# A gather for 144 tokens instead of 128, and the order of head 0's projections

## The chip, the cores and the metric

The kernel runs on one core of a Trainium2 chip. The metric is device time in microseconds (us) of one execution; the median of three executions of the kernel before is 3711.65 us (3703.98 to 3716.35). Engines go by the profile's names: PE is TensorE's matmul stream and PEld its weight loads, DVE is VectorE, ACT ScalarE, POOL GpSimd, SP SyncE.

## The reference

512 tokens of width 1024 pass through two blocks in fp32. Block one: convolution mixers, cross attention to 256 memory tokens, and a mixture of 16384 one-neuron experts:

```
q = h @ w_pq                          # 8 heads, two halves of 128
top 16 of each half's 128 scores; top 16 of their 256 sums -> expert_idx, gates
act = gelu(u[expert_idx] . h) * gates # 128 experts per token, rows of 1024
out = sum(act * v[expert_idx])
```

Block two puts 16 meta tokens in front (528 tokens) and runs a gated feed-forward layer, a hybrid mixer and a second feed-forward layer. The mixer has retention (4 heads, decayed scores) and sparse attention, whose keys are chosen by an index score: eight index heads of width 64, `sum_h w_h * relu(iq_h . ik)`, top 128 per query.

## The kernel before, in words

**Weights.** Every product of activations and weights is three matmuls (high times high, high times low, low times high). `_plan` lists all weight blocks of 1 MB in order of use. SP loads a block into one of three buffers (`wraw`, line 76); `_split` makes the high half on ScalarE (`whi`, line 95) and the low half on VectorE or GpSimd (`wlo`, line 96), each with two buffers. `K.mm` (line 175) issues the matmuls at line 184; weights are the stationary operand, tokens the moving one. One block is 16 steps of 3 matmuls.

**The list in the background.** Work of the other engines is put as pairs of a cost and a function into `K.bg`. After each step `K.step` (line 127) adds `K.rate` (times the share of 512 tokens that the matmul had) to a balance, and runs functions while it is positive. Costs are thus only a planned order; `flush` runs all that is left. `hold` and `wait` put an empty entry with a cost there.

**The experts.** The first NS = 128 tokens gather their experts' rows; for the other ND = 384 all experts are computed and most gates are zero. Dense part: `u_block` (line 888) multiplies 256 experts' first-layer rows with the 384 tokens, followed by GELU. 64 such blocks are 16 groups. The first 12 groups (spilled) run while the routing is still being done, and go to DRAM (`AD`, line 1080). Then, for each of the four last groups, `_peer_order` gives a fused pair (first layer, then second) and three second layers of spilled groups, which are reloaded (`back`, `reload`, lines 1099 to 1108): 4 first-layer and 16 second-layer groups, each of 4 blocks of 48 matmuls. `weigh` (line 1093) multiplies activations with the gates and splits them (lines 1096, 272, 274); `v_group` adds to the residual (line 1133). The gates come from `four` (line 1030): one-hot matrices of 4 tokens built on GpSimd, VectorE and ScalarE, and 4 matmuls (line 1058); `gather` (line 1046) brings 16 tokens' gates to DRAM (`GD`).

**The gathered tokens.** `_Gathered` (line 795) holds the 128 tokens with one token per partition. `rows_of_h` transposes their activations (line 811). 128 times per layer, `read` (line 819) issues an indirect DMA of one row per token (128 x 4 KB) on GpSimd's queue, and `step` (line 830) multiplies: for u a product with a sum per token (line 836), for v a scaled addition into `sum` (line 844). Four row buffers, two rows read ahead. These 256 steps stand in the list: `among` (line 847) puts EARLY = 30 + 30 + 38 among the `four`s of the three later token tiles, `more` (line 858) adds PACE = 2.4 per block of a first layer, 1.45 (and one more in a first block) where a spilled group is reloaded, 3.4 in other second layers. `finish` transposes `sum` back before the last group.

**Order on GpSimd's queue.** GpSimd issues, in program order, the row gathers, the reloads and the gates' loads, and builds most of the one-hots. Three buffers of `a` take the reloads; the fourth reload waits for the first to be weighed.

**The mixer around the change.** `_retention` (line 1302) projects the keys of head 0, the index key, the first four heads' index queries (w_iq[0], `proj` at line 1403, rope at line 1406), then half of head 0's values (line 1402, `_values` at line 1286), the other four's, and per head the query (line 1427), values, decayed scores (`inner`, line 1441), their product with the values (line 1464), gates and an output product. `index(i, hp)` (line 1355, 16 calls of 6 small matmuls, 2 relus and 2 sums) and 48 `drop`s (line 1376) stand in the list. Three PSUM accumulators (`mm`) serve projections, values and index products alike. After head 0's values the list is emptied down to its last 52 entries (line 1435):

```
for b in range(2):
    if b:
        values(0)
    o = proj(HQ)
```

Of the kernel before, what the change touches and what calls it, by code (L numbers as in the profile page):

```python
# [18 lines left out]
P = 128  # L19
D = 1024  # L20
# [10 lines left out]
NS = 128  # L31
# [5 lines left out]
EARLY = (30, 30, 38)  # L37
PACE = (2.4, 1.45, 3.4)
# [346 lines left out]
def _plan(d):  # L385
# [47 lines left out]
    add(d["w_iq"][0], True)  # L433
    add(d["w_rv"][0], True)
    add(d["w_iq"][1], True)
    for h in range(4):
        add(d["w_rq"][h], True)
        for n in ("w_rv", "w_rg"):
            for b in range(2):
                if (n, h, b) != ("w_rv", 0, 0):  # L440
                    add(d[n][2 * h + b], True)
# [353 lines left out]
class _Gathered:  # L795


    def __init__(self, K, tp, H):
        self.K, self.tp, self.H = K, tp, H
# [3 lines left out]
    def rows_of_h(self):  # L803

        nc = self.K.nc
        box = self.K.tp.tile([P, T2], F32, name="acc", tag="acc", bufs=1)
        self.gate, self.dots, self.index = box[:, :P], box[:, P:2 * P], box[:, 2 * P:3 * P].bitcast(U32)
        o = self.K.ps.tile([P, 1024], F32, name="mm", tag="mm", bufs=3)
        for k in range(KT):
            for i in range(2):  # L810
                nc.tensor.matmul(o[:, k * P:(k + 1) * P], self.H[i][:, k, :NS].bitcast(F32), self.K.ident, start=i == 0, stop=i == 1)
        nc.scalar.activation(self.h, o, AF.Copy)

    def begin(self, i, j):
        self.K.nc.vector.scalar_tensor_tensor(self.index, i, float(P), j, op0=OP.mult, op1=OP.add)  # L815
        for _ in range(NROW - 2):
            self.read()

    def read(self):
        n = self.nread  # L820
        if n == 2 * P:
            return
        t = self.tp.tile([P, D], F32, name="row", tag="row", bufs=NROW)
        src = self.K.d["u_rows"] if n < P else self.K.d["v_rows"]
        self.K.nc.gpsimd.indirect_dma_start(out=t, out_offset=None, in_=src,  # L825
                                            in_offset=bass.IndirectOffsetOnAxis(ap=self.index[:, n % P:n % P + 1], axis=0))
# [3 lines left out]
    def step(self):  # L830
        n, nc = self.ndone, self.K.nc
        s = n % P
        self.ndone += 1
        t = self.rows.pop(n)
        if n < P:
            nc.vector.tensor_tensor_reduce(t, t, self.h, 1.0, 0.0, OP.mult, OP.add, self.dots[:, s:s + 1])  # L836
            if s == P - 1:
# [464 lines left out]
def _retention(K, tp, H, HQ, R, RT, roots, BIAS, YD, w):  # L1302
    nc, tc = K.nc, K.tc
    with tc.tile_pool(name="ret", bufs=1) as rp:
# [95 lines left out]
        for b in range(2):  # L1400
            if b:
                values(0)
# [444 lines left out]
```

## Time and profile before

| | |
|---|---|
| median of three executions | 3711.65 us |
| the profiled execution | 3718.03 us, its span 3716.3 us |
| TensorE, VectorE, ScalarE, GpSimd busy | 97%, 63%, 38%, 32% of the span |
| weight loads busy | 88% |
| granted clock of TensorE, mean | 0.983 |
| DMA traffic | 583.37 MB, 157 GB/s |

The profile is one execution. A group of instructions has a line of the kernel, an engine, an operation, tiles out<-in, a count, busy time, the mean of one, and what ended the idle time before it. A wait names who waited for whom. The clock is the share of full speed granted to TensorE in a stretch. Matmuls are pipelined, so the duration of one is longer than the pitch from one to the next.

### The profile page before, as it was taken

The numbers are of one execution on the slowest core, as the hardware profiler recorded it, in microseconds if no ns is written. First come the engines' busy times: TensorE is split into PE (matmuls) and PEld (weight loads), VectorE is DVE, ScalarE is ACT, GpSimd is POOL, SyncE is SP. The second block draws the span as 40 slices with busy tenths as digits, with TensorE's granted clock in tenths as the row PEclk, the third lists the DMA queues.
The fourth block names the chain that finished last, engine by engine and source line by source line (L and its number), as shares of the span: only waits on it lengthen the run. The fifth ranks groups of instructions, "written<-read, shape, count | busy, mean of one in ns | idle before, by whom it ended". The sixth has DMA issues, their size and how long they took to land. (4 is left out here: it accounts for less than half of the span.)

```text
span 3716.3 us, 51006 instructions
## 1 busy us (share of the span) xinstructions
PE 3596.8 (97%) x20457; PEld 3269.4 (88%) x20457; DVE 2323.2 (63%) x4126; ACT 1422.8 (38%) x2306; POOL 1179.2 (32%) x940
## 2 busy tenths in 40 slices
PE   8999999998999999999999999989999999999998
PEld 6888788898999899989999999978898889888887
DVE  7896734698888868877887433457534254563334
ACT  4223434235677733323234222333333355442223
POOL 1002323304899934343530100032334333301001
PEclk9999999999999999999999999999999999999999
DMA  3223222236899988888884222231222221332221
GB/s 140 91 102 131 97 102 80 93 118 212 290 298 313 345 302 325 308 293 291 309 320 162 91 91 91 63 111 47 72 83 83 100 88 66 120 111 91 92 101 57
DMA packets 155261, 583.37 MB, mean 157 GB/s; under 512 B 12704, under 2 KB 64032, under 8 KB 112912
## 3 DMA queue, kind: packets, MB, share of 16 engines
q1 hardware_dynamic: 51456, 345.21, 26.5%
q0 software_dynamic: 46576, 190.34, 14.2%
q10 hardware_dynamic: 56992, 44.57, 3.7%
q8 instruction: 161, 2.64, 0.3%
q14 instruction: 76, 0.62, 0.1%
HBM read 527.63 MB, written 52.43 MB: 156 GB/s over the span
## 5 line engine op out<-in xcount | busy, mean ns | idle before, releaser
L184 PE MATMUL mm<-h,whi 128*128 128x512 f32 (+2 forms) x6944 | 1796.4, 351 | 14.4 <-ACT h L380 7.3
L184 PEld LDWEIGHTS mm<-h,whi 128*128 128x128 f32 x6944 | 1195.9, 190 | 146.5 <-ACT h L380 7.3
L184 PE MATMUL mm<-h,wlo 128*128 128x512 f32 (+2 forms) x3472 | 1134.7, 350 | 18.3 <-DVE wlo L96 17.3
L95 ACT ACTIVATE whi<-wraw 128x512 fp32r<-128x512 f32 (+2 forms) x648 | 654.6, 1041 | 524.9 <-PE mm L184 261.2
L184 PEld LDWEIGHTS mm<-h,wlo 128*128 128x128 f32 x3472 | 626.1, 190 | 89.7 <-DVE wlo L96 21.3
L96 DVE TENSOR_TENSOR wlo<-wraw,whi 128x512 fp32r<-128x512 f32 (+2 forms) x387 | 563.5, 1461 | 211.5 <-ACT whi L95 210.9
L96 POOL TENSOR_TENSOR wlo<-wraw,whi 128x512 fp32r<-128x512 f32 (+1 forms) x261 | 436.9, 1696 | 800.7 <-ACT whi L95 765.1
L184 PE MATMUL mm<-w,whi 128*128 128x384 f32 x2048 | 530.4, 340 | 1.4 <-ACT whi L95 1.2
L184 PEld LDWEIGHTS mm<-w,whi 128*128 128x128 f32 x2048 | 376.7, 190 | 2.6 <-ACT whi L95 1.9
L184 PE MATMUL mm<-w,wlo 128*128 128x384 f32 x1024 | 349.5, 341 | 21.0 <-DVE wlo L96 21.0
L1223 POOL TENSOR_TENSOR sl<-sl,r 128x528 f32<-128x528 f32 (+1 forms) x44 | 57.2, 1314 | 732.8 <-ACT sl L1221 732.8
L1037 POOL TENSOR_SCALAR p<-iota,it 128x128 f32<-128x128 f32 x256 | 253.1, 1000 | 44.5 <-ACT whi L95 31.9
L825 POOL DMA_INDIRECT row<-v_rows,acc x128 | 193.1, 1509 | 209.0 <-DVE sum L844 173.5
L184 PE MATMUL mm<-g,whi 128*128 128x264 f32 (+2 forms) x1080 | 226.4, 318 | 0.0
L825 POOL DMA_INDIRECT row<-u_rows,acc x128 | 164.2, 1283 | 176.7 <-DVE acc L815 108.2
L184 PEld LDWEIGHTS mm<-w,wlo 128*128 128x128 f32 x1024 | 194.9, 190 | 25.2 <-DVE wlo L96 25.2
L198 PE MATMUL mm<-whi,h 128*128 128x256 f32 x960 | 181.7, 285 | 7.4 <-DVE tmp L1261 2.6
L844 DVE SCALAR_TENSOR_TENSOR sum<-row,acc,sum 128x1024 f32<-128x1024 f32 x127 | 162.9, 1282 | 33.3 <-DMA row<-v_rows,acc 31.2
L184 PEld LDWEIGHTS mm<-g,whi 128*128 128x128 f32 x1080 | 166.8, 188 | 15.0
L836 DVE CUSTOM_DVE_ANT_0 row<-row,hrow 128x1024 f32<-128x1024 f32 x128 | 156.8, 1232 | 28.2 <-DMA row<-u_rows,acc 28.0
L272 ACT ACTIVATE w<-a 128x384 fp32r<-128x384 f32 x128 | 63.6, 526 | 262.9 <-DVE a L1096 259.2
L198 PEld LDWEIGHTS mm<-whi,h 128*128 128x128 f32 x960 | 151.7, 190 | 9.9 <-DVE v L1295 2.9
(376 smaller groups left out, 4414.5 us busy)
## 6 DMA issues: line engine op xcount, KB each, us to landing
wraw<-uT SPq DMA_DIRECT2D x64, 1024.0 KB, 6.9
wraw<-v SPq DMA_DIRECT2D x64, 1024.0 KB, 7.3
wraw<-w_in SPq DMA_DIRECT2D x27, 1024.0 KB, 4.8
gd<-gc ACTq DMA_DIRECT2D x24, 1024.0 KB, 10.0
g<-gd POOLq DMA_DIRECT2D x16, 1536.0 KB, 8.9
wraw<-ffn_w_gate SPq DMA_DIRECT2D x22, 1024.0 KB, 4.7
wraw<-ffn_w_up SPq DMA_DIRECT2D x22, 1024.0 KB, 4.7
ad<-a ACTq DMA_DIRECT2D x48, 384.0 KB, 7.1
```

The source lines that it names most:

```text
L95: self.nc.scalar.activation(hi[:, a:a + m], t[:, a:a + m], AF.Copy)
L96: eng.tensor_sub(lo[:, a:a + m], t[:, a:a + m], hi[:, a:a + m].bitcast(F32))
L184: self.nc.tensor.matmul(o, a[:, k, (c0 + c) * P:(c0 + c + 1) * P], b[:, k0 + k, lo:hi], start=first and k == 0 and i == 0, stop=last and k ...
L198: self.nc.tensor.matmul(out, x, y, start=start and i == 0, stop=stop and i == 2)
L272: self.nc.scalar.activation(dst[0], src, AF.Copy)
L825: self.K.nc.gpsimd.indirect_dma_start(out=t, out_offset=None, in_=src, in_offset=bass.IndirectOffsetOnAxis(ap=self.index[:, n % P:n % P + ...
L836: nc.vector.tensor_tensor_reduce(t, t, self.h, 1.0, 0.0, OP.mult, OP.add, self.dots[:, s:s + 1])
L844: nc.vector.scalar_tensor_tensor(self.sum, t, self.dots[:, s:s + 1], self.sum, op0=OP.mult, op1=OP.add)
L1037: eng.tensor_scalar(p2[:, j], IOTA, IT[1][:, t:t + 1], None, op0=OP.is_equal)
L1223: nc.gpsimd.tensor_mul(sl[c], sl[c], R)
```

## The change

NS becomes 144: 16 tokens more (NX) gather, and the dense part runs over 368 tokens. The 16 tokens have 16 x 128 expert rows; these are laid out as 128 partitions x 16 (SLOTS), eight partitions per token, so that one gather of 128 rows brings eight rows for each of the 16 tokens; 16 jobs per layer are added to 128, which makes 288 in all, in the order u of the 128 tokens, u of the 16, v of the 128, v of the 16. `begin_rest` sends the indices and gates of the 16 tokens through DRAM into that layout (four DMAs on GpSimd's queue, after the second token tile is routed). `rows_of_h(1)` repeats each of the 16 tokens eight times (ScalarE) and transposes again; `fold` adds the sum of the 128 tokens before the last 16 jobs, and `finish` adds up the eight partitions of each token with eight matmuls. EARLY, PACE and the rate while the spilled groups run are set anew.

In the mixer both index queries are projected in a row, and both halves of head 0's values follow the retention query, as in the other heads: the first half right behind it, the second behind the decayed scores. The plan's order of weights follows.

```
-NS = 128
+NS = 144
+NX = NS - 128
+SLOTS = 8 * 16 * NX // 128
-EARLY = (30, 30, 38)
-PACE = (2.4, 1.45, 3.4)
+EARLY = (30, 30, 40)
+PACE = (2.6, 1.85, 3.8)
...
+        self.jobs = [("u", 0, s) for s in range(P)] + [("u", 1, s) for s in range(SLOTS)]
+        self.jobs += [("v", 0, s) for s in range(P)] + [("v", 1, s) for s in range(SLOTS)]
...
+            if part:
+                for i in range(2):
+                    x[i] = K.temp().rearrange("p (k t) -> p k t", k=4)
+                    nc.scalar.activation(x[i].rearrange("p k (t h) -> p k t h", t=NX),
+                                         self.H[i][:, k0:k0 + 4, P:NS].bitcast(F32).unsqueeze(3).to_broadcast([P, 4, NX, P // NX]), AF.Copy)
...
+    def begin_rest(self, i, j, v, t):
+        nc = self.K.nc
+        d = self.K.dr.tile([2, NX, P], F32, name="rest")
+        nc.vector.scalar_tensor_tensor(t, i, float(P), j, op0=OP.mult, op1=OP.add)
+        nc.gpsimd.dma_start(d[0], t[:NX].bitcast(F32))
+        nc.gpsimd.dma_start(d[1], v[:NX])
+        for n, x in enumerate((self.index[1].bitcast(F32), self.gate[1])):
+            nc.gpsimd.dma_start(x, d[n].rearrange("t (h k) -> (t h) k", k=SLOTS))
...
+        if last and part == 0:
+            self.K.bg[:0] = [(0.3, lambda: self.rows_of_h(1))] if kind == "u" else [(2.0, lambda: None), (0.5, self.fold)]
...
-        while self.due >= 1 and self.planned < 2 * P:
+        while self.due >= 1 and self.planned < len(self.jobs):
...
+    def finish(self):
+        K, nc = self.K, self.K.nc
+        self.more(len(self.jobs))
+        K.flush()
+        a = K.aux()[:, :KT * NX].rearrange("p (k t) -> p k t", k=KT)
+        for k in range(KT):
+            nc.tensor.matmul(a[:, k], self.sum[:, k * P:(k + 1) * P], self.group, start=True, stop=True)
+        x = self.X[:, :, P:NS]
+        nc.vector.tensor_add(x, x, a)
...
+                if t == 1:
+                    rest.begin_rest(box[0], box[1], box["v"].rearrange("p h k -> p (h k)"), small("ix", U32, "t9"))
...
-            K.rate, K.fine, K.late = 0.64, True, True
+            K.rate, K.fine, K.late = 0.66, True, True
...
         for b in range(2):
-            if b:
-                values(0)
             o = proj(HQ)
...
             if b == 0:
-                K.wait(K.us(8.0))
+                K.wait(K.us(11.0))
...
-            values(0 if h else 1)
+            values(0)
...
-            if h:
-                values(1)
+            values(1)
```

## Rows read from the trace of the kernel before

**Rows 1.** The page, its first part: busy time, share of the span, instructions.

```profile
PE 3596.8 (97%) x20457; PEld 3269.4 (88%) x20457; DVE 2323.2 (63%) x4126; ACT 1422.8 (38%) x2306; POOL 1179.2 (32%) x940
```

**Rows 2.** Windows by stage, all engines (the first line names the columns).

```profile
core 0: us, PE busy (x) PEld busy (x) DVE busy (x) ACT busy (x) POOL busy (x), PEclk, DMA share, GB/s
764.00:887.00 123.00, 113.37 (x657) 110.96 (x656) 116.66 (x447) 49.87 (x88) 2.44 (x2) 0.99 0.40 138
887.00:1305.00 418.00, 403.59 (x2508) 398.21 (x2507) 350.01 (x861) 299.03 (x703) 374.97 (x354) 0.98 0.91 308
1305.00:2024.00 719.00, 689.55 (x3853) 682.64 (x3851) 570.22 (x670) 237.91 (x261) 268.61 (x220) 0.98 0.80 293
2441.50:2562.00 120.50, 105.22 (x574) 85.49 (x573) 75.39 (x143) 38.69 (x82) 32.60 (x24) 0.87 0.17 60
```

**Rows 3.** Windows of line 184 alone (PE, PEld, clock, DMA): widths 384, then 264.

```profile
1382.20:1482.80 100.60, 100.60 (x578) 100.60 (x577) 1.00 0.89 328
2100.00:2400.00 300.00, 300.00 (x2465) 300.00 (x2464) 1.00 0.26 87
```

**Rows 4.** Chain of waits, matmuls of width 512: start, us, what.

```profile
3340.58 359.51 PE mm L184 x1569
```

**Rows 5.** Groups of TensorE and VectorE, 887 to 1305 us: count, busy us, mean ns.

```profile
L1058 PE MATMUL aux<-p,p 128*128 128x128 f32 x768 | 109.4, 282 | 14.4 <-issue 7.8 <-DVE p L1042 3.1 <-POOL p L1037 3.1
L836 DVE CUSTOM_DVE_ANT_0 row<-row,hrow 128x1024 f32<-128x1024 f32 x98 | 121.1, 1235 | 22.7 <-DMA row<-u_rows,acc 22.5
```

**Rows 6.** TensorE in order of time where the list is flushed.

```profile
1301.03 3.98 PE L1058 MATMUL aux<-p,p 128*128 128x128 f32 x16 [6.09 <-issue]
```

**Rows 7.** Waits, 1305 to 2024 us, VectorE's and one of TensorE's: total, times, longest.

```profile
DVE a L1096 <- DMA a<-ad: 54.0, 11, 7.3
DVE wlo L96 <- ACT whi L95: 42.4, 38, 4.9
DVE sum L844 <- DMA row<-v_rows,acc: 31.2, 13, 5.9
DVE row L836 <- DMA row<-u_rows,acc: 5.5, 3, 3.7
PE mm L184 <- DVE wlo L96: 27.9, 16, 3.1
```

**Rows 8.** Groups of VectorE, 1305 to 2024 us: count, busy us, mean ns.

```profile
L96 DVE TENSOR_TENSOR wlo<-wraw,whi 128x2048 fp32r<-128x2048 f32 x80 | 183.1, 2289 | 42.5 <-ACT whi L95 42.4
L844 DVE SCALAR_TENSOR_TENSOR sum<-row,acc,sum 128x1024 f32<-128x1024 f32 x127 | 162.9, 1282 | 33.3 <-DMA row<-v_rows,acc 31.2
L274 DVE TENSOR_TENSOR w<-a,w 128x384 fp32r<-128x384 f32 x128 | 66.1, 557 | 11.8 <-ACT w L272 5.9
L1096 DVE TENSOR_TENSOR a<-a,g 128x384 f32<-128x384 f32 x128 | 65.4, 553 | 54.0 <-DMA a<-ad 54.0
L1133 DVE TENSOR_TENSOR X<-X,mm 128x384 f32<-128x384 f32 x126 | 63.8, 548 | 1.2 <-PE mm L184 1.1
```

**Rows 9.** Who waited for line 811's matmuls: us, times.

```profile
  ACT hrow L812: 5.3, 1
```

**Rows 10.** Window of the third second-layer group, which has no reload; columns as in rows 2.

```profile
1449.20:1482.80 33.60, 33.60 (x195) 33.60 (x194) 26.52 (x28) 8.60 (x7) 16.38 (x13) 1.00 0.90 338
```

**Rows 11.** Waits of TensorE, 2441.5 to 2562 us.

```profile
PE aux L198 <- DVE tmp L1449: 3.0, 1, 3.0
PE mm L198 <- DVE tmp L1261: 2.6, 1, 2.6
```

**Rows 12.** Groups, 2441.5 to 2562 us: the index matmuls and their sums.

```profile
L198 PE MATMUL mm<-ik,iq 64*128 64x128 f32 (+3 forms) x96 | 13.5, 377 | 6.7 <-DVE iq L1267 3.8 <-ACT iq L1265 2.9
L1369 DVE SCALAR_TENSOR_TENSOR sc<-rel,iw,sc 128x128 f32<-128x128 f32 (+3 forms) x28 | 17.4, 620 | 8.5 <-ACT rel L1365 6.6
```

**Rows 13.** Windows in the mixer, columns as in rows 2.

```profile
2500.00:2518.00 18.00, 18.00 (x81) 11.63 (x81) 11.58 (x21) 6.24 (x17) 4.73 (x3) 0.81 0.35 133
2544.00:2562.00 18.00, 17.78 (x61) 15.10 (x61) 3.63 (x10) 3.85 (x8) 0.00 (x0) 0.53 0.00 0
```

More of the change, by code (lines that the diff above doesn't have):

```diff
@@ L432, in _plan @@
     add(d["w_i"])
-    add(d["w_iq"][0], True)
-    add(d["w_rv"][0], True)
-    add(d["w_iq"][1], True)
+    for b in range(2):
+        add(d["w_iq"][b], True)
     for h in range(4):
@@ L795, with __init__ @@
 class _Gathered:
-    def __init__(self, K, tp, H):
-        self.K, self.tp, self.H = K, tp, H
+    def __init__(self, K, tp, H, X):
+        self.K, self.tp, self.H, self.X = K, tp, H, X
         self.h = tp.tile([P, D], F32, name="hrow", tag="hrow")
         self.rows, self.nread, self.ndone, self.planned, self.due = {}, 0, 0, 0, 0.0
[L803 to L811, printed above, removed]
+        self.jobs = [("u", 0, s) for s in range(P)] + [("u", 1, s) for s in range(SLOTS)]
+        self.jobs += [("v", 0, s) for s in range(P)] + [("v", 1, s) for s in range(SLOTS)]
@@ new lines, in rows_of_h @@
+    def rows_of_h(self, part=0):
+        nc, K = self.K.nc, self.K
+        if part == 0:
+            box = K.tp.tile([P, T2], F32, name="acc", tag="acc", bufs=1)
+            cut = [0, P, 2 * P, 3 * P] + [3 * P + i * SLOTS for i in (1, 2, 3)]
+            a = [box[:, x:y] for x, y in zip(cut, cut[1:])]
+            self.gate, self.dots, self.index = (a[0], a[3]), (a[1], a[4]), (a[2].bitcast(U32), a[5].bitcast(U32))
+            self.group = K.tp.tile([P, NX], F32, name="group")
+            nc.vector.tensor_reduce(self.group, K.ident.rearrange("p (t h) -> p t h", t=NX), AX.X, OP.add)
+        else:
+            self.h = self.tp.tile([P, D], F32, name="hrow", tag="hrow")
+        o = K.ps.tile([P, 1024], F32, name="mm", tag="mm", bufs=3)
+        for k0 in range(0, KT, 4):
+            x = [h[:, k0:k0 + 4, :P].bitcast(F32) for h in self.H]
+            if part:
[3 more added lines that the diff above has]
+                                         self.H[i][:, k0:k0 + 4, P:NS].bitcast(F32).unsqueeze(3).to_broadcast([P, 4, NX, P // NX]), AF.Copy)
+            for k in range(4):
+                for i in range(2):
+                    nc.tensor.matmul(o[:, (k0 + k) * P:(k0 + k + 1) * P], x[i][:, k], K.ident, start=i == 0, stop=i == 1)
@@ L819, in read @@
     def read(self):
         n = self.nread
-        if n == 2 * P:
+        if n == len(self.jobs):
             return
+        kind, part, s = self.jobs[n]
         t = self.tp.tile([P, D], F32, name="row", tag="row", bufs=NROW)
-        src = self.K.d["u_rows"] if n < P else self.K.d["v_rows"]
-        self.K.nc.gpsimd.indirect_dma_start(out=t, out_offset=None, in_=src,
-                                            in_offset=bass.IndirectOffsetOnAxis(ap=self.index[:, n % P:n % P + 1], axis=0))
+        self.K.nc.gpsimd.indirect_dma_start(out=t, out_offset=None, in_=self.K.d[kind + "_rows"],
+                                            in_offset=bass.IndirectOffsetOnAxis(ap=self.index[part][:, s:s + 1], axis=0))
@@ L863, in more, with fold @@
             self.due -= 1
-    def finish(self, X):
+    def fold(self):
         K, nc = self.K, self.K.nc
-        self.more(2 * P)
-        K.flush()
         for i in range(2):
@@ L885, in _peer @@
         HR = [x[:, :, NS:] for x in H]
[L886 removed]
+        rest = _Gathered(K, tp, H, X)
         def u_block(c_outer=True):
@@ L1070, in _peer @@
                 fours = [(1.1, lambda tb=tb, q=q: four(tb, q))
-                         for tb in range((t * P - NS) // TCH, ((t + 1) * P - NS) // TCH) for q in range(TCH // 4)]
+                         for tb in range(max(t * P - NS, 0) // TCH, ((t + 1) * P - NS) // TCH) for q in range(TCH // 4)]
                 if t < 3:
```

36 lines of the change are left out of this document (19 added, 17 removed).

## The prediction

> **What bounds the kernel now.** The first part of the page shows TensorE busy in 3596.8 of 3716.3 us [rows 1], so a gain has to come out of its matmuls or its few waits, and what matters is which engine it waits for in the two places that the change touches. The windows by stage cut these out [rows 2]. From 764 to 887 us (first three groups of the expert layer, with the routing) VectorE is busy 116.7 of 123 us. From 887 to 1305 us (the other nine spilled groups) TensorE is busy 403.6 of 418, GpSimd 375.0, VectorE 350.0, the DMA engines 0.91. From 1305 to 2024 us (fused groups and second layers) TensorE is busy 689.6 of 719 and VectorE 570.2. From 2441.5 to 2562 us (index queries up to the end of retention head 0's products) TensorE is busy only 105.2 of 120.5 us, at a granted clock of 0.87.
>
> Busy time does not say what is late, so the waits come next. From 1305 to 2024 us TensorE waits 27.9 us for VectorE's low halves of weights, while VectorE waits 54.0 us for reloads of spilled tiles and 31.2 and 5.5 us for rows, and 42.4 us for high halves on ScalarE, but 1.1 us for TensorE directly [rows 7, 8]. So in this stage VectorE's work plus its DMA waits, 570.2 + 90.7 = 660.9 us, is a second limit almost as long as TensorE's work.
>
> **Cheaper columns.** All 6144 matmuls of the expert layers get 368 columns for 384. Their pitch: 576 matmuls (three groups of 192) in 100.60 us, 175 ns; at 264 columns 2465 in 300 us, 122 ns [rows 3]; at 512, 1569 in 359.5 us, 229 ns [rows 4]. The slopes are 0.44 and 0.43 ns a column, and the shorter width is still on the line, so no weight load sets a floor at 368. Sixteen columns are worth 6.8 to 7.1 ns; I take 6.9. That is 15.9 us over the 2304 matmuls of the spilled groups and 26.5 us over the 3840 of the later ones, if TensorE sets the time there.
>
> The Trainium skill's page "TensorE: Matmul & The Clock Gate", section "Back-to-back issue gap", speaks against this: it says that both operations set the spacing and gives a stream of them a sustained 81 ns at 128 columns and 131 ns at 512, which is an estimated 2.1 ns for 16 columns and 12.8 us in all instead of 42.4. The trace disagrees at 512 columns (229 ns), and I go by the trace.
>
> **764 to 887 us: nothing.** VectorE leaves no room [rows 2], and its routing work is unchanged. The 4 us that TensorE saves in three groups become longer waits for low halves.
>
> **887 to 1305 us: -10 us.** 1728 matmuls save 11.9 us. Four calls of `four` go (23 blocks of 16 tokens, not 24), with 16 gather matmuls at 0.142 us, 2.3 us more [rows 5]. VectorE loses their one-hots and gains two row products of 1.24 us, GpSimd about the same, so neither gets more to do. Two things are added. By the costs written in the list, what is left for the flush at the end rises from 7.9 to 10.3 units, one `four` and one row product more; TensorE already stands still 6.1 us there [rows 6], and I add 2.5 us (two VectorE jobs of 1.24 us). And `begin_rest` puts four small DMAs on GpSimd's queue, the two reads behind the two writes' landing; behind them stand GpSimd's one-hots of the first `four`, which TensorE wants. No row shows that round trip; it lies between nothing (the pieces are two jobs ahead) and the 6.1 us of the flush, and I take 1.5, nearer to nothing because of that lead. Sum -14.2 + 4.0, about -10; bounds -14 and 0 (VectorE, GpSimd and the DMA engines let nothing go faster).
>
> **1305 to 2024 us: +8 us.** Row products in this stage rise from 158 to 188 (288 jobs less EARLY's 100, 256 less 98). Thirty at 1.282 us are +38.5 us of VectorE; its narrower operations give back 16/384 of 66.1 + 65.4 + 63.8 us, -8.1 [rows 8]. The second `rows_of_h` makes the next row product wait for 16 matmuls and a copy, as the first made ScalarE wait 5.3 us [rows 9]; I take 6 us with the fold of the first 128 tokens, which only moves forward, and the eight matmuls at the end. VectorE's own work becomes 570.2 + 36.4 = 606.6 us, and with the same 90.7 us of DMA waits 697.3 us. TensorE's side falls to 689.6 - 26.5 = 663.1. So VectorE becomes the longer chain, and the stage lasts 697.3 us plus what VectorE still spends stopped by the others. Before, that was 719 - 660.9 = 58 us. It arises where VectorE runs ahead and waits for the next high half, whose buffer TensorE holds. In a spilled group (12 of 20) it cannot run ahead any more: 8.4 row products (10.8 us), four low halves (9.2), and 8 each of the three narrow operations (11.8) are 31.7 us before any reload wait, against 192 matmuls of 168 ns, 32.2 us. The other 8 groups keep their share, 23 us. But where VectorE was stopped by TensorE, a reload had time to land; the 11 waits average 4.9 us, the longest is 7.3 [rows 7]. I add 7 us, a fifth of the way to 7.3 at all 12 reloads (33.6 us more). 697.3 + 30 = 727, +8 us. Bounds: -20 (TensorE sets the time: -26.5 + 6) and +42 (below). More rows also load GpSimd's queue: each gather still waits there for the buffer of the row product four before it, as now, and the reloads stand behind the gathers; what that costs is in the reload and row waits.
>
> **2441.5 to 2562 us: -18 us.** Before, the second index projection ends and its index products follow at once, so TensorE waits 6.7 us for the rope [rows 12]; now the retention query stands between, 48 matmuls of 229 ns, 11 us, about what a rope lasts. Before, head 0's decayed scores are wanted as soon as they are asked for, 3.0 us; now the second half of the values stands between. The values after the first index projection wait 2.6 us for an accumulator that a rope still reads [rows 11]; they move. Behind these waits the granted clock is 0.81 from 2500 to 2518 and 0.53 from 2544 to 2562 us, TensorE being busy in both [rows 13]: a mix of its 2.4 and 1.2 GHz levels that costs 0.19 x 18 + 0.47 x 18 = 11.9 us. That is 24.2 us. Against it: index products now start inside head 0's first values, by the costs nine of them, and the list is then emptied to 52, seven in one burst. The first may wait for the accumulator of the query's rope, 2.6 us as before. The burst is 42 matmuls of 0.141 us, 5.9 us, against 14 sums of 0.62 us on VectorE, 8.7 us [rows 12], so what follows on TensorE waits up to 2.8 us. I leave one short dip of the clock, 1 us. 24.2 - 6.4, about -18. Bounds -26 (every wait and dip goes) and -6 (the burst and new dips give most of it back). Masking work moved out of the values runs later, in heads whose VectorE is half idle; nothing. If it were late, attention's first scores would wait.
>
> **Sum.** 0 - 10 + 8 - 18 = -20 us against the profiled execution's 3718.0 us, which is 6.4 us above the median of the three runs. From the median, 3711.65 - 20 = 3692 us.
>
> **The rivals.** *TensorE still sets the time from 1305 us on*: -20 there, -48 in all, 3664 us. For it: three groups in a row ran at the full pitch without a stall [rows 3], and VectorE was stopped 42.4 us waiting for high halves [rows 7]. Against it: the 31.7 us above, without a wait.
>
> *Slower: row products and reloads become the chain of the fused stage.* Place: VectorE between the reload's issue and its first use. Price: all 12 reloads at 7.3 us (87.6 for 54.0), row waits in proportion to 188 rows for 158 (43.7 for 36.7), 23 us of slack: 606.6 + 131.3 + 23 = 761, +42 us, in all +14, 3726 us. It decides from +39 on, where it outweighs both gains by 0.3%. For it: DMA engines 0.90 busy at 338 GB/s in a group with 3.4 rows a block [rows 10], which now gets 3.8 in less time. Against: most reload waits were below 7.3.
>
> The Trainium skill's "DMA: Bandwidth & Descriptors", "Specifications", limits a core to about 358 GB/s from HBM; the 3.8 rows of 0.52 MB and 1.05 MB of weights would need an estimated 8.5 us a block by it. The trace is at 338 there, so it agrees that little is left.
>
> *The mixer keeps its stalls*: the burst, accumulators and dips give back all but 6 us; -10 + 8 - 6 = -8, 3704 us. For it: ScalarE, VectorE and TensorE meet in the burst. Against: nothing is left that waits for a rope just begun.
>
> *The narrower matmul is no faster, its weight load setting the pitch*: nothing for 16 columns leaves +2 before 1305 us (4.0 - 2.3), +8 and -18, -8 in all, 3704 us. For it: every matmul has its load, and the loads' row is busy 682.6 of 719 us [rows 2]. Against: 122 ns at 264 columns, each with its load too [rows 3].
>
> **How the numbers follow.** Chances: forecast 0.50, TensorE-bound 0.17, slower 0.13, mixer 0.16, weight loads 0.04. A measurement of this kernel can tell about 0.3%, 11 us. The forecast's own range is 3674 to 3708, about 0.85 of it beyond -11 us; with all of the TensorE-bound case and a fifth of the mixer's that gives 0.63 for faster; slower is most of its case, 0.11; the rest, 0.26, is same. The range 3670 to 3718 leaves out half of the TensorE-bound case and most of the slower one.
>
> **What would show it.** Right: matmuls of 368 columns at 168 ns in unstalled stretches; the stage after the flush about as long as before, with VectorE's reload waits nearer 7 us and fewer waits on high halves; from the first index projection to head 0's last product about 102 us, without the 6.7 and 3.0 us waits. Wrong: a fused stage shorter by 15 us or more (VectorE was not the chain), or longer by 25; TensorE idle again in the index burst; the first `four` late by more than 5 us.

## The result and the profile after

The change made the kernel **slower**: 3730.97 us, median of 9 runs (3721.19 to 3739.07), against 3711.65 us (9 runs, 3702.45 to 3720.78) before; ratio 1.0057, interval 1.0041 to 1.0072. The forecast was 3692. The profiled execution took 3730.97 us (span 3729.2), so its span stands 12.9 us above that of before.

The span, cut at the first and last matmul of each part (us, from the two traces):

| part | before | after | difference | forecast |
|---|---|---|---|---|
| front, up to the expert layer | 764.0 | 749.1 | -14.9 | 0 |
| first three spilled groups | 123.1 | 121.5 | -1.6 | 0 |
| nine spilled groups | 417.6 | 419.6 | +2.0 | -10 |
| fused stage | 718.7 | 772.4 | +53.7 | +8 |
| up to the end of head 0's products | 538.6 | 521.1 | -17.5 | -18 |
| the rest | 1154.3 | 1145.6 | -8.7 | 0 |

Two steps held (the first three groups and the mixer), two failed, and two parts whose code did not change got shorter. Profiles of one kernel differ too: a second execution of the kernel before (e0 below) has 413.3 us in the nine spilled groups, 714.6 in the fused stage and 534.4 in the fifth part, each some 4 us less than here. So single differences of 4 to 6 us between profiles say little. First part of the page after, then the windows of the four stages (columns as in [rows 2]):

```profile
PE 3547.3 (95%) x20473; PEld 3238.2 (87%) x20473; DVE 2351.5 (63%) x4162; ACT 1415.2 (38%) x2292; POOL 1235.0 (33%) x968
```

```profile
749.00:870.50 121.50, 110.58 (x657) 108.31 (x657) 116.41 (x447) 49.34 (x88) 3.07 (x2) 0.96 0.39 139
870.50:1290.00 419.50, 390.66 (x2474) 381.74 (x2473) 345.10 (x849) 290.70 (x683) 374.23 (x352) 0.97 0.90 304
1290.00:2062.50 772.50, 690.89 (x3900) 677.59 (x3900) 602.12 (x720) 238.81 (x267) 325.75 (x251) 0.94 0.80 292
2483.00:2583.70 100.70, 94.24 (x576) 80.20 (x575) 70.66 (x132) 39.58 (x84) 31.39 (x24) 0.93 0.21 74
```

The third line against [rows 2] is the whole case. VectorE's busy time rose from 570.2 to 602.1 us, as the sum had it (606.6). TensorE's did not fall, 689.6 to 690.9, though its matmuls are narrower, while its granted clock fell from 0.98 to 0.94; and it stood still 81.6 us instead of 29.5.

The narrow matmul is as fast as forecast. Line 186 (184 before) in an undisturbed stretch, columns as in [rows 3]:

```profile
1834.00:1862.00 28.00, 28.00 (x168) 27.56 (x167) 1.00 0.89 326
```

28.00 us for 168 is 167 ns, against 175 [rows 3].

The waits of the fused stage, answering to [rows 7] (total, times, longest):

```profile
PE mm L186 <- DVE wlo L98: 57.5, 26, 6.6
DVE a L1140 <- DMA a<-ad: 56.7, 10, 8.0
DVE wlo L98 <- ACT whi L97: 37.1, 36, 4.4
DVE sum L873 <- DMA row<-v_rows,acc: 26.6, 12, 5.7
DVE row L865 <- DMA row<-u_rows,acc: 15.0, 5, 4.5
DVE X L1177 <- PE mm L186: 10.3, 4, 4.8
PE mm L828 <- ACT tmp L824: 9.4, 1, 9.4
DVE row L865 <- ACT hrow L829: 8.2, 1, 8.2
```

VectorE's groups there, answering to [rows 8] (count, busy us, mean ns):

```profile
L98 DVE TENSOR_TENSOR wlo<-wraw,whi 128x2048 fp32r<-128x2048 f32 x80 | 183.1, 2289 | 37.1 <-ACT whi L97 37.1
L873 DVE SCALAR_TENSOR_TENSOR sum<-row,acc,sum 128x1024 f32<-128x1024 f32 x142 | 182.2, 1283 | 29.4 <-DMA row<-v_rows,acc 26.6
L276 DVE TENSOR_TENSOR w<-a,w 128x368 fp32r<-128x368 f32 x128 | 64.3, 544 | 9.0 <-ACT w L274 3.0
L1140 DVE TENSOR_TENSOR a<-a,g 128x368 f32<-128x368 f32 x128 | 63.3, 536 | 56.7 <-DMA a<-ad 56.7
L1177 DVE TENSOR_TENSOR X<-X,mm 128x368 f32<-128x368 f32 x126 | 61.7, 531 | 10.3 <-PE mm L186 10.3
```

Reload and row waits add up to 98.3 us, against 90.7 before and 97.7 forecast. What rose is TensorE's wait for low halves, 27.9 to 57.5 us, and behind such a wait comes half clock. One of them, columns as in [rows 2]:

```profile
1493.00:1496.60 3.60, 0.00 (x0) 0.00 (x0) 3.60 (x5) 1.36 (x1) 0.94 (x1) 1.00 0.42 132
1498.00:1501.30 3.30, 3.30 (x12) 3.30 (x11) 3.27 (x5) 0.00 (x0) 2.88 (x2) 0.50 0.81 298
```

TensorE stands 3.6 us while VectorE is busy throughout; 1.4 us after it the clock is granted at 0.50 (1.2 of 2.4 GHz) and a full TensorE starts 10 matmuls in 3.3 us (the 12 counted include two begun before), where 20 would fit. Over the fused stage the stretches at half clock add up to 28 us before and 85 us after, at a cost of half their length. So: 3840 matmuls at 167 ns are 641 us, plus 82 of waits, plus 42 of clock, is 765 of the 772. Before: 672 + 29 + 14 = 715 of 719.

### The profile page after: what moved, and what is told of

It is laid out like the page before. It is cut to its first block, busy times and chain, and to the rows that moved or that the text cites. A ratio compares the mean times of both kernels' runs of the same rounds, so it can differ in the third digit from the quotient of the medians.

```text
span 3729.2 us, 51104 instructions
## 1 busy us (share of the span) xinstructions
PE 3547.3 (95%) x20473; PEld 3238.2 (87%) x20473; DVE 2351.5 (63%) x4162; ACT 1415.2 (38%) x2292; POOL 1235.0 (33%) x968
## 5 line engine op out<-in xcount | busy, mean ns | idle before, releaser
L186 PE MATMUL mm<-h,whi 128*128 128x512 f32 (+2 forms) x6944 | 1768.5, 348 | 17.5 <-ACT h L382 8.2
L186 PE MATMUL mm<-h,wlo 128*128 128x512 f32 (+2 forms) x3472 | 1123.2, 346 | 28.9 <-DVE wlo L98 28.5
L186 PE MATMUL mm<-w,whi 128*128 128x368 f32 x2048 | 525.2, 338 | 6.7 <-ACT whi L97 4.2
L186 PE MATMUL mm<-w,wlo 128*128 128x368 f32 x1024 | 349.0, 341 | 42.9 <-DVE wlo L98 42.8
L852 POOL DMA_INDIRECT row<-v_rows,acc x144 | 225.5, 1566 | 191.1 <-DVE sum L873 155.6
L852 POOL DMA_INDIRECT row<-u_rows,acc x144 | 189.0, 1312 | 199.0 <-DVE acc L832 107.0
L865 DVE CUSTOM_DVE_ANT_0 row<-row,hrow 128x1024 f32<-128x1024 f32 x144 | 176.9, 1239 | 48.5 <-DMA row<-u_rows,acc 40.2
L873 DVE SCALAR_TENSOR_TENSOR sum<-row,acc,sum 128x1024 f32<-128x1024 f32 x142 | 182.2, 1283 | 29.4 <-DMA row<-v_rows,acc 26.6
L274 ACT ACTIVATE w<-a 128x368 fp32r<-128x368 f32 x128 | 61.7, 512 | 312.9 <-DVE a L1140 306.3
L513 DVE SCALAR_TENSOR_TENSOR co<-cf,convw,co 128x511 f32<-128x511 f32 (+14 forms) x240 | 157.5, 730 | 0.2 <-ACT co L511 0.2
```

The source lines that it names most:

```text
L186: self.nc.tensor.matmul(o, a[:, k, (c0 + c) * P:(c0 + c + 1) * P], b[:, k0 + k, lo:hi], start=first and k == 0 and i == 0, stop=last and k ...
L274: self.nc.scalar.activation(dst[0], src, AF.Copy)
L513: nc.vector.scalar_tensor_tensor(CO[:, k, s:], CF[:, k, :S - s], cw, CO[:, k, s:], op0=OP.mult, op1=OP.add)
L873: nc.vector.scalar_tensor_tensor(self.sum, t, dots[:, s:s + 1], self.sum, op0=OP.mult, op1=OP.add)
```

## Experiments

Each kernel was compared with the kernel before on the same chip. "Fused" is the length of the fused stage in the profile.

### The two parts of the change apart

e1 is the kernel before with the mixer's and the load list's part; e2 is the kernel after without that part; e0 is the kernel before, unedited.

```diff
-    add(d["w_iq"][0], True)
-    add(d["w_rv"][0], True)
-    add(d["w_iq"][1], True)
+    for b in range(2):
+        add(d["w_iq"][b], True)
...
-            if b:
-                values(0)
             o = proj(HQ)
...
```

> The kernel before, once more, for a profile from the same chip as the next three. Theory (the loss lies in the fused stage): its fused stage lasts about 719 us again, and a 512-column matmul has one pitch in this profile and in those of the other three. Rival (the two profiles shown so far differ because they come from different executions, 233 against 227 ns at 512 columns): the stages of this profile differ from the first by 10 us or more.

> The kernel before with the mixer part alone. Theory: the mixer part is a gain by itself, about 18 us, 0.995 of before, all of it between the first index projection and head 0's product of scores and values. Rival (it only looks so in one profile, and gives it back in the later heads): within 5 us of before.

> The changed kernel with the mixer's old order: the 144 gathered tokens alone. Theory: the whole loss and more lies here, about 38 us slower than before (20 measured and 18 that the mixer gives), 1.010. Rival (the loss lies in the mixer's order or in both together): within 10 us of before.

Measured: e0 1.0003 (0.9990 to 1.0016), e1 **0.9950** (0.9932 to 0.9969), e2 **1.0103** (1.0081 to 1.0125). The mixer's part is a gain of about 18 us and the gathering, as the change makes it, a loss of about 38. (e2 has the gain of a shifted layout in it, next section; without that the gathering costs more, e7 at 1.0120 against e1 at 0.9950.) In the table's fifth part e1 has 519.6 us, e0 534.4, e2 535.7. In the kernel after, TensorE's waits from the first index projection on, answering to [rows 11]:

```profile
PE mm L200 <- ACT rel L1409: 3.1, 5, 1.3
PE mm L200 <- POOL wlo L98: 1.5, 2, 1.3
PE mm L200 <- DVE tmp L1322: 1.4, 1, 1.4
```

The 6.7 us for the rope [rows 12] are gone and the index burst gives back 3.1 and one dip: from 2522 us the clock is at half for 10.2 us, behind waits of 1.3 and 1.4. Head 0's products now run at full clock, where [rows 13] had 0.53:

```profile
2564.00:2582.00 18.00, 18.00 (x139) 17.47 (x138) 11.44 (x33) 7.08 (x15) 5.06 (x4) 1.00 0.17 59
```

### Why unchanged code got faster: 64 bytes

All kernels with 144 tokens had a shorter front and rest. Their `group` tile takes 64 bytes a partition in the temps pool, ahead of the pool that holds H. e4 gives the kernel before (with the mixer's part) such a tile; e7 takes it out of the way in the kernel after.

e4:

```diff
+        nc.vector.memset(self.K.tp.tile([P, 16], F32, name="pad"), 0.0)
```

e7:

```diff
-            cut = [0, P, 2 * P, 3 * P] + [3 * P + i * SLOTS for i in (1, 2, 3)]
+            cut = [0, P, 2 * P, 3 * P] + [3 * P + i * SLOTS for i in (1, 2, 3)] + [3 * P + 3 * SLOTS + NX]
-            self.group = K.tp.tile([P, NX], F32, name="group")
+            self.group = a[6]
```

> The kernel before with the mixer part of the change alone, and one tile more of 64 bytes a partition in the temps pool (where the change has its group tile), written once and never read; 128 tokens gather, as before. Theory (the change shortened code that it doesn't touch because that tile moves what lies behind it by 64 bytes): 512-column matmuls go from 233-234 ns to 227, the front gets 12 us shorter, what follows the mixer's head-0 sums 9 us, and the 384-column matmuls gain some ns as well; about 21 us or more off the mixer part alone, 0.989 of before or less. Rival (the gain comes from something else of the 144-token program): 0.995, as the mixer part alone, with 233-234 ns.

> The kernel after with its group tile laid inside the tile that holds gates and indices, so that nothing behind it in the temps pool moves by 64 bytes; the same instructions otherwise. Theory (layout): 512-column matmuls back at 233 ns, the front back at 762 us, the part behind the mixer's head-0 sums at 1154, the whole about 20-30 us slower than after, 1.011-1.014 of before. Rival (the gain comes from something else of the 144-token program): 1.005-1.006, as after.

Measured: e4 **0.9904** (0.9873 to 0.9934), 3667.7 us; e7 **1.0120** (1.0094 to 1.0147), 3750.8 us. Front and rest: e4 750.8 and 1145.3 us, e7 760.6 and 1154.1. The chain's stretch of 1569 matmuls of 512 columns ([rows 4]) in the kernel after, in e4 and in e7:

```profile
3363.11 349.59 PE mm L186 x1569
```

```profile
3300.14 349.59 PE mm L184 x1569
```

```profile
3374.09 359.51 PE mm L186 x1569
```

349.59 with the 64 bytes, 359.51 without, to the hundredth, whichever kernel. Of the 1569 matmuls 57 have 256 columns (118 ns without, 120 with the 64 bytes); the 1512 of 512 columns take 233 ns without and 227 with them. That the layout does it is shown; what in the addresses does it was not tried. e4 computes everything and beats both kernels.

### Narrow matmuls against VectorE's load

e6 is the kernel after with narrower tiles only. e8 and e9 are e4 and e6 with three quarters of each later row product left out.

e6:

```diff
-EARLY = (30, 30, 40)
-PACE = (2.6, 1.85, 3.8)
+EARLY = (30, 30, 38)
+PACE = (2.4, 1.45, 3.4)
...
-        self.jobs = [("u", 0, s) for s in range(P)] + [("u", 1, s) for s in range(SLOTS)]
-        self.jobs += [("v", 0, s) for s in range(P)] + [("v", 1, s) for s in range(SLOTS)]
+        self.jobs = [(kind, 0, s) for kind in "uv" for s in range(P)]
...
```

`begin_rest`, the second product of H's rows and the eight matmuls of `finish` go with them.

e9 (e8 has the same in the older kernel's names):

```diff
+            w = D if n < sum(EARLY) else D // 4
-            nc.vector.tensor_tensor_reduce(t, t, self.h, 1.0, 0.0, OP.mult, OP.add, dots[:, s:s + 1])
+            nc.vector.tensor_tensor_reduce(t[:, :w], t[:, :w], self.h[:, :w], 1.0, 0.0, OP.mult, OP.add, dots[:, s:s + 1])
...
-            nc.vector.scalar_tensor_tensor(self.sum, t, dots[:, s:s + 1], self.sum, op0=OP.mult, op1=OP.add)
+            w = D // 4
+            nc.vector.scalar_tensor_tensor(self.sum[:, :w], t[:, :w], dots[:, s:s + 1], self.sum[:, :w], op0=OP.mult, op1=OP.add)
```

> The kernel after with narrower tiles only: the 16 further tokens are left out of the 384-now-368-column stages and no rows are gathered for them (no second product of H's rows, no further jobs, no folding back by group), paces as before. Theory (the columns saved are a real gain of 7-8 ns a matmul, and the row work of the 16 tokens eats it): fused stage 718 - 30 = 685-695 us, spill stage 887-1305 shorter by at most 10 us, since GpSimd's one-hots pace it; the whole 0.980-0.985 of before with the mixer's and the layout's gain. Rival (VectorE and the reloads pace the fused stage, and a faster TensorE only waits more): fused stage 710 us or more, waits for low halves 40 us or more.

> The kernel before with the mixer part and the 64-byte pad (e4), where VectorE's row products behind the first 98 jobs are done on a quarter of each row (256 of 1024 elements); it leaves out the rest of those rows. The gathers are whole. About 158 products get some 0.9 us shorter, so VectorE loses about 140 of its 571 us in the fused stage. Theory (VectorE sets when the low halves come, and TensorE's waits and half clock follow): fused stage from 718 to 675-690 us, waits for low halves from 32 to under 12 us. Rival (the reloads and the gathers on GpSimd's queue set it): fused stage 705 us or more.

> The same quarter-width products in the narrower kernel without the 16 tokens' rows (e6); it leaves out those tokens' rows and three quarters of the later ones. Theory: with VectorE's load gone, the narrower matmuls give what their pitch says, 3840 x 6.6 ns = 25 us: fused stage 650-668 us, 20-28 us below the same with 384 columns, where the whole products left 7 us of it. Rival (something else than VectorE swallows the columns' gain): 12 us or less below the same with 384 columns.

The fused stage's windows of e4, e6, e8 and e9, in this order (columns as in [rows 2]):

```profile
1280.70:1999.00 718.30, 685.10 (x3851) 678.87 (x3851) 571.49 (x674) 237.91 (x261) 271.42 (x220) 0.98 0.81 295
```

```profile
1288.00:2000.00 712.00, 667.46 (x3870) 659.58 (x3868) 568.18 (x680) 237.54 (x266) 275.79 (x220) 0.97 0.80 293
```

```profile
1281.20:1967.00 685.80, 676.36 (x3855) 673.70 (x3854) 451.05 (x674) 237.92 (x261) 217.56 (x222) 0.99 0.83 310
```

```profile
1278.50:1945.00 666.50, 651.26 (x3850) 647.55 (x3849) 443.30 (x674) 234.73 (x261) 213.37 (x221) 0.99 0.84 316
```

Ratios 0.9904, 0.9888 (0.9864 to 0.9911), 0.9796 (0.9771 to 0.9821) and 0.9750 (0.9724 to 0.9776). With whole products, sixteen columns less are worth 7 us of the 25 us that 3840 matmuls at 6.5 ns give: the rival of e6's expectation. With quarter products they are worth 19 us, a little under what theory asked (20 to 28). GpSimd's gathers and the DMA engines carry the same rows in all four (DMA share 0.80 to 0.84); only VectorE's load differs. So **VectorE paces the fused stage**, and most of what TensorE saves turns into waiting for it: 33 us of waits in e4, 43 in e6, 9 in e8, 15 in e9.

### What the sixteen tokens' rows cost

Four kernels take a part of them away. e3: no second product of H's rows. e5: the gathers without VectorE's products. e10: e5 and no second product of H's rows. e12: e6 with the change's paces, so the same 256 jobs planned more densely, and no gather more.

e3, e10:

```diff
-            self.K.bg[:0] = [(0.3, lambda: self.rows_of_h(1))] if kind == "u" else [(2.0, lambda: None), (0.5, self.fold)]
+            self.K.bg[:0] = [] if kind == "u" else [(2.0, lambda: None), (0.5, self.fold)]
```

e5:

```diff
-            nc.vector.tensor_tensor_reduce(t, t, self.h, 1.0, 0.0, OP.mult, OP.add, dots[:, s:s + 1])
+            if part == 0 or s == 0:
+                nc.vector.tensor_tensor_reduce(t, t, self.h, 1.0, 0.0, OP.mult, OP.add, dots[:, s:s + 1])
+                if part:
+                    nc.vector.memset(dots[:, 1:], 0.0)
...
-        else:
+        elif part == 0:
             nc.vector.scalar_tensor_tensor(self.sum, t, dots[:, s:s + 1], self.sum, op0=OP.mult, op1=OP.add)
```

e12, on e6:

```diff
-EARLY = (30, 30, 38)
-PACE = (2.4, 1.45, 3.4)
+EARLY = (30, 30, 40)
+PACE = (2.6, 1.85, 3.8)
```

> The changed kernel without the second transposition: the 16 tokens' row products take the 128 tokens' activations, so that computation is left out. Theory (this one meeting of VectorE, ScalarE and TensorE costs far more than the 6 us that I gave it): 13 to 17 us faster than the changed kernel, about 1.001 of before. Rival (TensorE's wait there is only moved, VectorE being the chain anyway): 3 us faster or less, 1.005.

> The kernel after, without the VectorE row products of the 32 jobs of the 16 further tokens but the first of each kind; their gathers, the second product of H's rows, fold and finish stay. It leaves out those 16 tokens' weighted rows. Theory (VectorE's added work makes the low halves late, and each wait pulls the clock down): 30 products of about 1.2 us fall away, TensorE's waits for low halves in the fused stage go from 57 us to about 30, half-clock time from 85 to 30-45 us, the fused stage from 772 to 720-735 us, the whole to 0.993-0.997 of before. Rival (the 32 gathers and the second product of H's rows cost it, by queueing in front of the reloads): fused stage 755 us or more, 1.002 or more.

> The kernel after without the 16 tokens' products (e5) and without the second product of H's rows as well, so that of the 16 tokens' rows only the 32 gathers, their places in the list of background steps and the folds are left. It leaves out those tokens' rows. Without the products the fused stage took 745 us, without gathers too 712 us. Theory (the second product of H's rows, with the chain dot, gelu, expansion, TensorE, copy, cost most of that): 712-722 us. Rival (the 32 gathers and their places in the list, behind which reweighing and reloads come later, cost it): 733 us or more.

> The narrower kernel that gathers no rows for the 16 tokens (e6; it leaves those rows out), with the paces of the change: the same 256 jobs, planned more densely into the groups, done some groups earlier. No gather and no product more than in e6 (fused stage 712 us). Theory (not the 32 further gathers as such but the denser row products in each group make VectorE late where it also reweighs): fused stage 735-755 us, waits for low halves 45-60 us, as in the kernel that had the 32 gathers without their products. Rival (the gathers in GpSimd's queue ahead of the reloads): 708-718 us.

| kernel | products in the stage | VectorE busy | TensorE's waits | at half clock | fused | ratio |
|---|---|---|---|---|---|---|
| e6 | 158 | 565 | 43 | 48 | 712 | 0.9888 |
| e12 | 156, denser | 565 | 64 | 57 | 740 | 0.9974 (0.9961 to 0.9987) |
| e5 | 158, denser | 568 | 66 | 57 | 745 | 1.0006 (0.9988 to 1.0023) |
| e10 | 158, denser | 566 | 67 | 77 | 750 | 0.9979 (0.9964 to 0.9994) |
| e3 | 188 | 601 | 79 | 83 | 766 | 1.0053 (1.0036 to 1.0070) |
| after | 188 | 602 | 82 | 85 | 772 | 1.0057 |

e3's theory fell: without the second product of H's rows the stage is 6 us shorter and the time about the same (1.0053 against 1.0057), not 13 to 17 us less. e5 came out between its two expectations. e10's theory fell as well: leaving out the second product in e5 made the stage no shorter (750 against 745; by the ratios, 0.9979 against 1.0006, it may have saved up to 10 us in all). So something else of the gathering costs most of the 33 us between e6 and e5, without a product more. e12 names it: 28 of these come from the **denser plan alone**, with no gather and no product added. Its window against e6's (above) shows VectorE with the same work in a longer stage; then TensorE's wait for low halves in e6 and in e12:

```profile
1288.50:2028.00 739.50, 675.60 (x3852) 663.66 (x3852) 564.51 (x670) 235.40 (x261) 274.64 (x219) 0.96 0.78 283
```

```profile
PE mm L186 <- DVE wlo L98: 37.1, 18, 5.2
```

```profile
PE mm L186 <- DVE wlo L98: 52.7, 23, 6.9
```

e12's last three reweighing groups have no product left, and take 32.0 to 32.1 us, undisturbed; those before them, with 7 to 10 products, take 35.1 to 47.5. In e6 five reweighing groups with 6 or 7 products take 32.0 too, and none with 8 or more. Why the same products cost 28 us more when packed this way is not shown beyond that. The last 30 products cost 28 us more (e5 to after), for 34 us of VectorE's busy time.

### Attempts to mend it

e13 and e14 give GpSimd the low halves of one block in four, in e4 and in the kernel after. e15 and e16 spread the products evenly over the groups, in e4 and after. e17 moves them out of the twelve groups in which VectorE also reweighs a spilled group.

e13, e14:

```diff
-            add(d["uT"][4 * g + b] if kind == "u" else d["v"][4 * g + b])
+            add(d["uT"][4 * g + b] if kind == "u" else d["v"][4 * g + b], b == 2)
```

e15, on e4:

```diff
-PACE = (2.4, 1.45, 3.4)
+PACE = (2.6, 1.6, 2.5)
```

e16:

```diff
-PACE = (2.6, 1.85, 3.8)
+PACE = (2.9, 2.1, 2.7)
```

e17:

```diff
-PACE = (2.6, 1.85, 3.8)
+PACE = (3.2, 1.45, 4.6)
```

> The kernel before with the mixer part and the 64-byte pad (e4), where GpSimd instead of VectorE makes the low halves of one block in four of the fused stage (20 blocks of 80: 2.4 us each on VectorE, about 5 us on GpSimd by the one whole-block row of the trace). It computes everything. Theory (VectorE paces the fused stage): VectorE's 571 us fall by about 45, the fused stage from 718 to 690-705 us, the whole to 0.983-0.987 of before. Rival (GpSimd's queue, where the gathers and reloads wait behind the 5 us): fused stage 718 us or more.

> The kernel after with the same 20 blocks' low halves on GpSimd. It computes everything. Theory: fused stage from 772 to 730-750 us, waits for low halves from 57 to about 35 us, the whole to 0.994-1.000 of before, so no slower than before but still above e13. Rival (GpSimd's queue is the limit with 32 gathers more): 765 us or more.

> The kernel before with the mixer part and the 64-byte pad (e4), with the same 158 row products of the fused stage spread evenly over its groups: 2.6, 1.6 and 2.5 jobs a block for the three kinds of group, in place of 2.4, 1.45 and 3.4. It computes everything. In e4 the groups planned at 3.4 a block (some 12 products) and the ones behind them hold most of the waits (42.2, 40.6 and 39.7 us for v5, u14 and u15 against 33.3 us undisturbed). Theory (VectorE's load within a group decides, not its mean): fused stage from 718 to 700-712 us. Rival (the mean load and the reload waits decide): 715-725 us. The whole at 0.985-0.989 or at 0.990.

> The kernel after with its 188 row products of the fused stage spread evenly (2.9, 2.1 and 2.7 a block in place of 2.6, 1.85 and 3.8). It computes everything. Theory (load within a group): fused stage from 772 to 750-762 us, the whole about 1.001-1.003 of before. Rival (every group is loaded beyond what fits beside its matmuls, however they are spread): 768-780 us, 1.005 or more.

> The kernel after with its 188 row products of the fused stage moved out of the 12 groups in which VectorE also reweighs a spilled group: those get 1.45 a block as before the change (after: 1.85), the four computed groups 3.2 (2.6) and the three groups ahead of one 4.6 (3.8). It computes everything. The even spread, 2.1 in the reweighing groups, made the stage 22 us longer. Theory (a reweighing group has no room for more than the 6 or 7 products it had; the other groups do): fused stage from 772 to 740-760 us, the whole 0.998-1.002 of before. Rival (whatever the spread, 188 products are too many): 768 us or more, 1.005 or more.

Measured: e13 0.9895 (0.9879 to 0.9912), fused 719 us; e14 1.0107 (1.0086 to 1.0127), 784 us; e15 0.9912 (0.9895 to 0.9928), 717 us; e16 1.0141 (1.0121 to 1.0162), 795 us; e17 1.0074 (1.0058 to 1.0091), 778 us. None mends it: all five theories fell, and e16 came out beyond its rival too. In e13 VectorE hands over 20 subtractions, 46 us, but its busy time falls by only 23. Its row additions take the other half back: some last up to 5.5 us, all of them while GpSimd subtracts. In e4, then in e13:

```profile
L843 DVE SCALAR_TENSOR_TENSOR sum<-row,acc,sum 128x1024 f32<-128x1024 f32 x127 | 162.9, 1283 | 34.0 <-DMA row<-v_rows,acc 31.7
```

```profile
L843 DVE SCALAR_TENSOR_TENSOR sum<-row,acc,sum 128x1024 f32<-128x1024 f32 x127 | 184.5, 1453 | 48.6 <-DMA row<-v_rows,acc 46.5
```

What is left goes into its DMA waits, the reloads' from 49.8 us in e4 to:

```profile
DVE a L1095 <- DMA a<-ad: 67.1, 10, 8.0
POOL wlo L96 <- ACT whi L95: 51.8, 9, 27.4
PE mm L184 <- POOL wlo L96: 7.8, 6, 2.1
```

GpSimd's queue issues the reloads too, and the subtraction on it waits for its high half, up to 27.4 us with the reloads and gathers behind it. In e16 and e17 the waits move with the products: with eleven or twelve products a reweighing group lasts 44 to 47 us in e16, and 57.5 where the second product of H's rows falls into it (an undisturbed one 32.0). In e17 the reweighing groups that kept five to seven take 32 to 39 us, but those of 14 and 15 ahead of them take 39 to 47, and three reweighing groups get eleven all the same, left over from there. So in none of the three spreads was there room for what the change adds; each only decided where TensorE waits.

### The nine spilled groups

e11 is e6 with 64 of GpSimd's 248 one-hots on VectorE (the expectation says 28 of 241; the edit moves one of each four's three, and the trace counts 184 left).

```diff
-                    eng = nc.gpsimd if j < (3 if t0 < 2 * P else 2) else nc.vector
+                    eng = nc.gpsimd if j < 2 else nc.vector
```

> The narrower kernel without the 16 tokens' rows (e6), where one of the three one-hots that GpSimd makes of each four of the first tokens goes to VectorE (28 of 241, 1.03 us each on GpSimd, 0.34 us on VectorE). Theory (GpSimd's one-hots pace the spill stage, so that it kept its 407-409 us although its matmuls got narrower): stage shorter by 5-12 us, 397-404 us, with TensorE's waits for GpSimd's one-hots from 10 us to under 4. Rival (VectorE or the DMA queues, at a share of 0.93, pace it): 407 us or more.

TensorE's waits there in the kernel after, in e6 and in e11:

```profile
PE aux L1102 <- POOL p L1081: 15.4, 15, 4.8
PE aux L1102 <- DVE p L1086: 8.4, 5, 3.0
```

```profile
PE aux L1094 <- POOL p L1073: 10.5, 17, 2.0
PE aux L1094 <- DVE p L1078: 6.1, 7, 2.5
```

```profile
PE aux L1094 <- POOL p L1073: 3.8, 4, 1.9
PE aux L1094 <- DVE p L1078: 10.3, 10, 2.8
```

Measured: 0.9861 (0.9834 to 0.9889), not told apart from e6's 0.9888; the part took 403.0 us against 409.2 in e6. That is what the theory asked, and the waits for GpSimd's one-hots fell to 3.8 us as it said, but 6 us for some 60 us of GpSimd's work is little. So GpSimd, busy 375 of 418 us before and 374 of 419.5 after, held the stage up, by some 6 us; what holds it then was not tried (the waits for VectorE's one-hots rise from 6.1 to 10.3 us). At one layout e4 has 407.3 us here and e6 409.2: sixteen columns less gave nothing.

The kernel after is 10 us above e6, and most of that stands in one place, its first `four`. GpSimd, then TensorE:

```profile
878.23 1.10 POOL L844 DMA_DIRECT2D acc<-rest  x2 [3.22 <-DMA rest<-ix]
880.85 0.80 PE L1102 MATMUL aux<-p,p 128*128 128x128 f32 x2 [4.77 <-POOL p L1081]
```

The reads of `begin_rest` stand 3.2 us on GpSimd's queue until its writes have landed, the one-hots stand behind them, TensorE waits 5.4 us for these, and 6.8 us at half clock begin at the end of the wait. The group of 192 matmuls in which this falls lasts 48.7 to 50.2 us in every kernel with `begin_rest` (49.3 in after), and 40.8 to 42.7 us in e6, e9, e11 and e12, which have the same columns and not `begin_rest`.

## Why the prediction was wrong, step by step

- **Cheaper columns: right.** 6.9 ns were forecast; at the same layout 384 columns take 173.3 ns (a group of 192 in e4 in 33.28 us) and 368 take 166.8 (32.03 us in e6), 6.5 ns. The prediction's row at 512 columns was misread: 57 of the 1569 matmuls of [rows 4] have 256 columns, so 512 take 233 ns, not 229, and the slope is 0.46 ns a column, not 0.43; little hangs on it. By the sustained figures of the Trainium skill's "TensorE: Matmul & The Clock Gate", section "Back-to-back issue gap", it would have been an estimated 2.1 ns; the measurement decides against them here.
- **764 to 887 us, nothing: right**, -1.6 us.
- **887 to 1305 us, -10: wrong**, +2.0. Two terms failed. One is the saving of 14.2 us, which rested on "GpSimd about the same, so neither gets more to do": that left the engines with as much to do as before, and at one layout sixteen columns less gave nothing (e4 407.3, e6 409.2). The other is `begin_rest`, put at 1.5 us, "nearer to nothing because of that lead": the lead did not cover it, and it cost 5.4 us of waits and 3.4 us of clock. The sign of being wrong that the prediction named, the first `four` late by more than 5 us, came about. Waits for GpSimd's one-hots rose from 3.1 to 15.4 us in all and half clock from 13 to 24.
- **1305 to 2024 us, +8: wrong**, +53.7, and this decided the sign. Term by term: VectorE's own work 606.6 forecast, 602 measured; DMA waits 97.7 and 98.3; the second product of H's rows 6, which e3 and e10 place between nothing and some 10. What failed is the slack, "what VectorE still spends stopped by the others". The text let it fall from 58 to 23 us because VectorE "cannot run ahead any more". It rose to 772.4 - 602.0 - 98.3 = 72 us. VectorE still waited 37.1 us for high halves, and 10.3 us for TensorE instead of 1.1. By the code these conversions stand on ScalarE's queue behind those of the reweighed tiles, and these wait for VectorE, so an engine that is late delays its own supply (argued from the code's order; ScalarE's wait for reweighed tiles rose from 259 to 306 us). A chain that is summed engine by engine leaves that out. What the runs show in place of +8: narrower matmuls -7 us (before to e6), the denser plan +28 (e12), gathers and second product without products +5 (e5), the 30 products +28.
- **The same step left out the clock.** TensorE's side was priced at 689.6 - 26.5 = 663.1 us, all at the clock of before. Its waits grew by 52 us and the half clock behind them by 57 us, 28 us lost: more than the narrower matmuls saved. The text had priced such dips in the mixer and nowhere else.
- **Group by group the shortage was seen and not priced.** "31.7 us before any reload wait, against 32.2" means that a spilled group has no room for the reload wait of some 5 us. The text counted reload waits in the sum of the whole stage, and put 7 us on their growth; e12 shows that the same work packed as the change packs it costs 28.
- **2441.5 to 2562 us, -18: right**, -17.5 in the table's part, by the waits it named; in the size there is some luck. The dips of the clock, of which it counted 11.9 us, were longer in that execution than in e0's (30.7 us at half clock against 20.5), and against e0's profile the part gained 13.3 us. The ratio of e1 says 18.
- **The slower rival came nearest in size (+42 for +53.7) but not in mechanism.** It wanted reload waits of 87.6 us; they were 56.7. The TensorE-bound rival is refuted by e6, the weight-load rival by the 166.8 ns, the one in which the mixer keeps its stalls by e1.
- **Unforeseen: the layout**, -15 and -9 us in parts that the change does not touch, of which the 64 bytes make 11.5 and 8.5 (e7 to after); the rest lies between executions (764.0 us before, 762.1 in e0). Without it the kernel is at 1.0120 (e7).

## What to carry to other kernels

In this stage two engines were each filled to over 90%, counting their waits for DMAs. Less work on one was worth little, 7 of 25 us. On the other, 30 products more of 1.28 us cost 28, but the plan that packed the work to make room for them cost as much again, and with all that came with them it was 60 (712 to 772). So count such a stage group by group and not by its mean. Price a wait of TensorE with the half clock behind it. And before a few microseconds in untouched code are put down to a change, give the kernel before the same layout: one tile of 64 bytes was worth some 20 us here (e7 against after), as much as the reordered mixer.

## Not expected of the hardware

- Moving the tiles behind one pool by 64 bytes a partition changes the pitch of 512-column matmuls from 233 to 227 ns. That of 384 columns stays: 173.3 ns in undisturbed groups of e0 and e1, without it, and of e4, with it.
- In e13, 14 of VectorE's 127 row additions ran while GpSimd subtracted a block; they took 2.83 us on average and up to 5.52, the other 113 took 1.28. In e14 it was 13 of 142, 2.60 us on average. The subtraction itself took about what e13's expectation had (5 us; 2.29 on VectorE):

```profile
L96 POOL TENSOR_TENSOR wlo<-wraw,whi x20: 4546/4640/5514, 1293.2 to 1975.9; 128x2048 fp32r<-128x2048 f32 x20
```
